# Two encoder layers on one core: the last placements of the recurrence's scores are traced later, and the sums over features are ordered behind the low half of their operand

## The chip, the cores and the metric

One core of a Trainium2 chip runs the whole program in one launch. The time is the device time of one execution in microseconds (us). The kernel before took 1623.28 us (median of 3 runs, 1622.96 to 1624.02).

## The reference

`x` is 512 tokens by 1024 features, and there are two layers. In each, a normed `x` goes through one wide projection (6144 columns) into a differential attention, a bidirectional gated recurrence (HGRN2) and two gates; both branches are projected, gated, summed, projected again and added to `x`; a SwiGLU feed-forward with 2816 hidden units follows. The change touches only the recurrence. For each of its 4 heads (128 features, 512 tokens) and each direction, the reference does this in chunks of 64 tokens:

```python
b = jnp.cumsum(gc, axis=2)
inter = jnp.einsum('bhck,bhkv->bhcv', qc * jnp.exp(b), state)
diff = b[:, :, :, None, :] - b[:, :, None, :, :]
decay = jnp.exp(jnp.where(tril[:, :, None], diff, -jnp.inf))
scores = jnp.einsum('bhtk,bhsk,bhtsk->bhts', qc, kc, decay)
intra = jnp.einsum('bhts,bhsv->bhtv', scores, vc)
```

and sums the outputs of the two directions, norms them over the head's features and multiplies them with a sigmoid gate.

## The kernel before, in words

Everything is feature-major: 128 features on the partitions, 512 tokens along the free axis. The projections split each fp32 operand into a high and a low fp32r half (`hi`, `lo`, or `hh`, `hl`) and run three matmuls per block of 128 features (`mm3`, lines 208 to 210); the high half is made by ScalarE (line 92, a copy), the low half by VectorE (`tt`, line 81, a subtraction). These matmuls are the rows `m<-...`.

`hgrn_head` computes one head. Both directions go through one 128x512 matrix of scores `A` (key tokens by query tokens, in four blocks of 128). As the decay between two tokens cannot be had as a product over a whole chunk, the pairs of tokens are split into levels. Level L (64, 32, 16, 8, 4, 2) covers the pairs that lie in neighbouring blocks of L tokens. `level(L)` makes its two factors in one tile (`fl`): four VectorE subtractions or additions of 128x256 (`subs`), one ScalarE Exp over 128x1024 (`exp`), one VectorE product with `q` of 128x512 (`mult`); at L = 64 the pieces are a little different. `scores` multiplies the factors, four fp32 matmuls of 128x128 into one PSUM bank (`sc`; the trace has two records for each). `place` copies those entries of the bank that belong to the level into `A`: for L of 64, 32 and 16 by ScalarE copies of rectangles (lines 549, 553), and below by one VectorE predicated copy of 128x512 with a mask (line 556). Below level 2 there are two more terms, neighbours (1) and the diagonal (0), which are sums over the features of `kk`: `kk` is split into `kh` (ScalarE, line 574) and `kl` (VectorE, line 575, shown under line 81), each multiplied by a matrix of ones (`nr`, lines 580 and 581: 2 terms x 2 halves, 512 columns each), and placed by two more predicated copies. So a head has five predicated copies: 8, 4, 2, 1, 0. Then `po` (line 593) multiplies `A` and the chunk states with the values.

In this text sc(8), mult(2), place(4) and so on stand for the scores, the product and the placement of a level.

The loop before computes the factors of a level, then the scores of the level before it, and places these at once. After the loop it makes `kh` and `kl`, the scores of level 2, place(2), and the sums.

What sets the order. The instructions are not run in the order in which they are traced. A planner goes through the whole program at compile time, with its own estimates of durations, and for each engine picks among the instructions whose inputs are ready the one traced first; what stands in an `urgent()` block (loads, weight splits and evacuations of the projections) goes ahead. The result is a fixed queue per engine, which the engine works off in order, waiting on semaphores. So the heads, whose instructions depend on each other, are interleaved with projection matmuls that are independent of them. `behind(a, b)` tells the planner to order `a` after `b` although `a` does not use its result; it adds no semaphore. In `scores`, `mark` is the instruction after which the matmuls are ordered: the Exp of the next level, or for level 2 the copy to `kh`.

Two pools matter. The factor tiles (`tag="fac"`) have `FAC` = 4 slots. Two of them hold the factors of the chunk states (`ff`, `fb`) until `po`; the levels, `kh` and `kl` take turns in the other two, so `kl` takes the slot of level 2 and `kh` that of level 4, and the next head's `ff` and `fb` (the rows `fs`) take those of `kh` and `kl`. The PSUM banks of the heads come from a pool of 4 (`pside`). Heads run in two pairs per layer, and the eight heads are counted 0 to 7 here; even heads are first of a pair.

Of the kernel before, what the change touches and what calls it, by code (L numbers as in the profile page):

```python
# [9 lines left out]
F32 = mybir.dt.float32  # L10
# [4 lines left out]
ALU = mybir.AluOpType  # L15
# [32 lines left out]
def kernel(  # L48
# [17 lines left out]
    PE, DVE, ACT, POOL = nc.tensor, nc.vector, nc.scalar, nc.gpsimd  # L66
# [3 lines left out]
    def act(o, i, func, bias=None, scale=None, accum=None):  # L70
        kw = {}
        if bias is not None:
            kw["bias"] = bias
        if scale is not None:
            kw["scale"] = scale
        if accum is not None:
            kw["accum_out"] = accum
        return ACT.activation(o, i, func, **kw)  # L78

    def tt(o, a, b, op):  # L80
        return DVE.tensor_tensor(o, a, b, op)  # L81

    def stt(o, a, s, b, op0, op1):
        return DVE.scalar_tensor_tensor(o, a, s, b, op0, op1)  # L84
# [9 lines left out]
    def behind(ins, other):  # L94

        tc.add_manual_dep(ins.ins, other.ins.name,
                          mybir.DependencyInfo(mybir.DependencyClass.NoSync, mybir.DependencyReason.DATA),
                          reason="keep the tensor engine from waiting")
# [8 lines left out]
    def bank(name="s"):  # L107
        return pside.tile([P, T], F32, tag="s", name=name)

    def mbank(name="m"):  # L110
        return pm.tile([P, T], F32, tag="m", name=name)
# [6 lines left out]
    ones_r = cp.tile([P, P], F32R, name="ones_r")  # L118
# [261 lines left out]
    def sigmoid(v):  # L380

        act(v, v, AF.Exp, scale=-1.0)
        act(v, v, AF.Ln, bias=one)
        return act(v, v, AF.Exp, scale=-1.0)
# [21 lines left out]
    def hgrn_head(l, h, q, z, sg, vB, oh, ol, hgp):  # L406
# [28 lines left out]
        kk = z  # L435
# [47 lines left out]
        def turned(f, kc):  # L483

            pt = bank("kt")
            for i in range(3):
                c = (kc + i) * P
                PE.transpose(pt[:, i * P:(i + 1) * P], f[:, 1, c:c + P], ident)
            kt = hgp.tile([P, 3, P], F32, tag="kt", name="kt")
            return kt, ACT.copy(kt.rearrange("p i c -> p (i c)"), pt[:, :3 * P])  # L490

        def states(d, kt, kc, *marks):
            ps = bank("st")
            for i in range(3):
                mm = PE.matmul(ps[:, i * P:(i + 1) * P], kt[:, i, :], vB[:, kc + i, h * P:(h + 1) * P],
                               start=True, stop=True)
                for mark in marks:
                    behind(mm, mark)
            S = hgp.tile([P, 3, P], F32, tag=f"S{d}", name="S")
            order = (0, 1, 2) if d == 0 else (2, 1, 0)  # L500
            for n, i in enumerate(order):
                if n == 0:
                    DVE.tensor_copy(S[:, i, :], ps[:, i * P:(i + 1) * P])
                else:
                    stt(S[:, i, :], S[:, order[n - 1], :], dec[:, d, kc + i:kc + i + 1],
                        ps[:, i * P:(i + 1) * P], ALU.mult, ALU.add)
            return S

        def level(L):

            f = hgp.tile([P, 2, T], F32, tag="fac", name="fl", bufs=FAC)
            Q, K = blocks(f[:, 0, :]), blocks(f[:, 1, :])
            if L == 64:
                side = lambda v, i: v.rearrange("p (b two) c -> p b two c", two=2)[:, :, i]
                of, ob = [tot[:, d].rearrange("p (b two) -> p b two", two=2)[:, :, 0:1].to_broadcast([P, 4, 64])
                          for d in range(2)]
                act(side(Q, 1), side(cf, 1), AF.Exp)
                act(side(K, 1), side(ab, 1), AF.Exp)
                tt(side(Q, 0), ob, side(xb, 0), ALU.subtract)
                tt(side(K, 0), side(af, 0), of, ALU.add)  # L520
                act(side(Q, 0), side(Q, 0), AF.Exp)
                mark = act(side(K, 0), side(K, 0), AF.Exp)
            else:
                side = lambda v, i: v.rearrange("p b (n two c) -> p b n two c", two=2, c=L)[:, :, :, i]
                mid = lambda v: side(v, 0)[:, :, :, L - 1:L].to_broadcast([P, 8, 32 // L, L])
                of, ob = mid(cf), mid(cb)
                tt(side(Q, 1), side(cf, 1), of, ALU.subtract)
                tt(side(K, 1), side(ab, 1), ob, ALU.subtract)
                tt(side(Q, 0), ob, side(xb, 0), ALU.subtract)
                tt(side(K, 0), side(af, 0), of, ALU.add)  # L530
                mark = act(f, f, AF.Exp)
            tt(f[:, 0, :], f[:, 0, :], q, ALU.mult)
            return f[:, 1, :], f[:, 0, :], mark
# [4 lines left out]
        def scores(K, Q, mark):  # L538
            ps = bank("sc")
            for s in range(TC):  # L540
                c = slice(s * P, (s + 1) * P)
                mm = PE.matmul(ps[:, c], K[:, c], Q[:, c], start=True, stop=True)  # L542
                behind(mm, mark)
            return ps.rearrange("p (i c) -> p i c", c=P), mm

        def place(L, pv):

            if L == 64:
                ACT.copy(A, pv)
            elif L >= 16:  # L550
                for i in range(64 // L):
                    c = slice(i * 2 * L, (i + 1) * 2 * L)
                    ACT.copy(A[c, :, c], pv[c, :, c])
            else:
                j = (2 * L).bit_length() - 1 if L else 0
                DVE.copy_predicated(A, masks[:, j, :].unsqueeze(1).to_broadcast([P, TC, P]), pv)
# [3 lines left out]
        kf, _ = turned(ff, fk)  # L560
        kb, turn = turned(fb, bk)

        done = None
        for L in (64, 32, 16, 8, 4, 2):
            *kq, mark = level(L)
            if L == 32:
                behind(act(dec, suf[:, :, :, 0], AF.Exp), turn)
                S = [states(0, kf, fk, turn, mark), states(1, kb, bk, turn, mark)]
            if done is not None:
                place(done[0], scores(*done[1], mark)[0])  # L570
            done = (L, kq)
        kh = hgp.tile([P, 2, T], F32R, tag="fac", name="kh", bufs=FAC)
        kl = hgp.tile([P, 2, T], F32R, tag="fac", name="kl", bufs=FAC)
        mark = ACT.copy(kh, kk)
        tt(kl, kk, kh.bitcast(F32), ALU.subtract)
        pv, mark = scores(*done[1], mark)
        place(2, pv)
        for i in (1, 0):
            ps = bank("nr")
            behind(PE.matmul(ps, ones_r, kh[:, i, :], start=True, stop=False), mark)  # L580
            PE.matmul(ps, ones_r, kl[:, i, :], start=False, stop=True)
            place(i, ps.rearrange("p (i c) -> p i c", c=P))
        po = bank("po")
        last = None
        for c in range(TC):
            tok = slice(c * P, (c + 1) * P)
            terms = [(vB[:, c, h * P:(h + 1) * P], A[:, c, :])]
            if c < TC - 1:
                terms.insert(0, (S[1][:, c, :], fb[:, 0, tok]))
            if c > 0:  # L590
                terms.insert(0, (S[0][:, c - 1, :], ff[:, 0, tok]))
            for i, (a, b) in enumerate(terms):
# [6 lines left out]
        with tc.issue_after(first.ins):  # L599
            mark = sigmoid(sg)  # L600
# [114 lines left out]
    for l in range(LAYERS):  # L715
        win = w_in[l]
        an = [vecs[:, V_FFN + 8 * l + c:V_FFN + 8 * l + c + 1] for c in range(DC)]
        with ExitStack() as mix:
# [19 lines left out]
            with tc.tile_pool(name=f"hgrn{l}", bufs=2, reuse_waits="tile") as hgp:  # L738
# [22 lines left out]
                def run(h):  # L761
                    hgrn_head(l, h, *heads[h], vB, obh[:, h, :], obl[:, h, :], hgp)
# [59 lines left out]
        with tc.tile_pool(name=f"ffn{l}", bufs=2, reuse_waits="tile") as fp:  # L822
            gh = fp.tile([P, FC, T], F32R, name="gh", bufs=1)
            gl = fp.tile([P, FC, T], F32R, name="gl", bufs=1)
            for f0 in range(0, FC, 2):
# [3 lines left out]
                for f in (f0, f0 + 1):  # L829
                    c0 = slice((f - f0) * P, (f - f0 + 1) * P)  # L830
                    tmp = []
                    for raw in (rg, ru):
                        with urgent():
                            wh, wl = wsplit(raw[:, :, c0])
                        ps = mbank()
# [14 lines left out]
            if l < LAYERS - 1:  # L850
                nn = [vecs[:, V_ATT + 8 * (l + 1) + c:V_ATT + 8 * (l + 1) + c + 1] for c in range(DC)]
                for c0 in range(0, DC, 2):
                    ps = [mbank(), mbank()]
# [16 lines left out]
            else:  # L870
# [10 lines left out]
                ps = [[mbank(), mbank()] if t < 2 else [bank(), bank()] for t in range(TC)]  # L881
# [66 lines left out]
```

## Time and profile before

| | |
|---|---|
| median of 3 runs | 1623.28 us |
| the profiled execution | 1623.66 us, its span 1621.9 us |
| ACT busy, share of the span | 771.6 us, 48% |
| POOL busy | 8.1 us, 1% |
| DMA | 142.53 MB, mean 88 GB/s |
| granted TensorE clock, mean | 0.999 |

The profile shows one execution. PE is the matmul unit, PEld its weight loads, DVE VectorE, ACT ScalarE. PE's busy time counts overlapping matmuls, so a busy PE can still be late; how late is read from the distance between the starts of successive matmuls. A row of the timeline has start, duration, engine, line, operation, and in brackets how long the engine was idle ahead of it and for whom.

### The profile page before, as it was taken

To read this page: it belongs to the slowest core of one execution; us is meant where nothing else is said; L and a number is where in the kernel's file an instruction comes from. 1 tells how busy PE (TensorE), PEld (TensorE's weight loads), DVE (VectorE), ACT (ScalarE), POOL (GpSimd) and SP (SyncE) were. 2 spreads that over 40 slices of the span, in tenths; PEclk is the share of its full clock that TensorE was granted. 3 is DMA by queue.
4 is the path that set the end of the run, shared out by engine and by line. 5 is a ranking of instruction groups with operands and counts; after the bars stand their busy time and mean duration, and the time that the engine had idled before them with its cause. 6 is when DMAs were issued, how large, how long until landed. Compare 5 with 4: busy or idle time off the path is not lost.

```text
span 1621.9 us, 18719 instructions
## 1 busy us (share of the span) xinstructions
PE 1602.1 (99%) x7456; PEld 1323.5 (82%) x7456; DVE 1013.1 (62%) x1636; ACT 771.6 (48%) x1186; POOL 8.1 (1%) x21
## 2 busy tenths in 40 slices
PE   8999999999999999999999999999999999999998
PEld 6888888887888888888888888888878888888886
DVE  8878977877654444433368789788875444444224
ACT  4666666676432323322355667676754323233213
POOL 2000000000000000000000000000000000000000
PEclk9999999999999999999999999999999999999999
DMA  5312212221333223323322222122123233332221
GB/s 189 105 52 79 79 61 70 78 79 52 104 104 92 90 83 99 111 89 100 103 92 83 73 78 79 54 77 79 52 79 97 84 104 104 104 103 92 104 85 72
DMA packets 117927, 142.53 MB, mean 88 GB/s; under 512 B 3152, under 2 KB 100432, under 8 KB 117840
## 3 DMA queue, kind: packets, MB, share of 16 engines
q1 hardware_dynamic: 117152, 140.78, 26.8%
q8 instruction: 58, 0.95, 0.2%
q10 hardware_dynamic: 688, 0.56, 0.1%
q14 instruction: 29, 0.24, 0.0%
HBM read 139.23 MB, written 2.10 MB: 87 GB/s over the span
## 4 chain that ended last, share of the span: by engine, by line
PE 83%; DVE 11%; ACT 4%; issue 1%; DMA 0%; ACTq 0%; DVEq 0%
PE m L210 24%; PE m L208 24%; PE m L209 24%; DVE lo L81 2%; DVE fl L81 2%; PE sc L542 2%; PE s L208 1%; PE s L209 1%; PE s L210 1%; DVE z L81 1%; PE qk L659 1%; PE wt L706 1%; PE po L593 1%; PE qk L656 1%; DVE cum L447 1%
## 5 line engine op out<-in xcount | busy, mean ns | idle before, releaser
L92 ACT CAST hi<-raw 128x1024 fp32r<-128x1024 f32 (+2 forms) x274 | 272.2, 995 | 616.4 <-PE m L209 477.2
L208 PE MATMUL m<-hh,hi 128*128 128x512 f32 x1216 | 476.5, 392 | 5.7 <-DVE hi L289 5.7
L210 PE MATMUL m<-hh,lo 128*128 128x512 f32 x1216 | 476.2, 392 | 0.0
L209 PE MATMUL m<-hl,hi 128*128 128x512 f32 x1216 | 476.1, 392 | 0.0
L81 DVE TENSOR_TENSOR lo<-raw,hi 128x1024 fp32r<-128x1024 f32 (+2 forms) x282 | 320.9, 1139 | 177.5 <-ACT hi L92 176.1
L208 PEld LDWEIGHTS m<-hh,hi 128*128 128x128 f32 x1216 | 228.9, 188 | 52.2 <-ACT sacc L78 5.7
L209 PEld LDWEIGHTS m<-hl,hi 128*128 128x128 f32 x1216 | 228.9, 188 | 47.3 <-DVE hl L84 0.4
L210 PEld LDWEIGHTS m<-hh,lo 128*128 128x128 f32 x1216 | 228.9, 188 | 47.1 <-DVE lo L81 0.3
L81 DVE TENSOR_TENSOR gu<-m,rbc 128x512 f32<-128x512 f32 x88 | 60.9, 692 | 241.2 <-PE m L210 237.2
L208 PE MATMUL m<-hi,hh 128*128 128x512 f32 x256 | 101.4, 396 | 0.0
L209 PE MATMUL m<-lo,hh 128*128 128x512 f32 x256 | 100.9, 394 | 0.0
L210 PE MATMUL m<-hi,hl 128*128 128x512 f32 x256 | 100.9, 394 | 0.0
L78 ACT ACTIVATE fl<-fl 128x1024 f32<-128x1024 f32 (+1 forms) x56 | 48.5, 872 | 43.8 <-DVE fl L81 43.8
L210 PE MATMUL m<-gh,lo 128*128 128x512 f32 x176 | 68.5, 389 | 0.0
L209 PE MATMUL m<-gl,hi 128*128 128x512 f32 x176 | 68.5, 389 | 0.0
L208 PE MATMUL m<-gh,hi 128*128 128x512 f32 x176 | 68.5, 389 | 0.0
L210 PEld LDWEIGHTS m<-hi,hl 128*128 128x128 f32 x256 | 48.2, 188 | 9.6
L542 PEld LDWEIGHTS sc<-fl 128*128 128x128 f32 x384 | 49.0, 191 | 8.5 <-DVE fl L81 4.3
L209 PEld LDWEIGHTS m<-lo,hh 128*128 128x128 f32 x256 | 48.2, 188 | 9.3
L208 PEld LDWEIGHTS m<-hi,hh 128*128 128x128 f32 x256 | 48.2, 188 | 9.3
L542 PE MATMUL sc<-fl 128*128 128x128 f32 x384 | 51.5, 277 | 2.8 <-DVE fl L81 2.6
L209 PE MATMUL m<-ml,hi 128*128 128x512 f32 x128 | 49.8, 392 | 0.0
(255 smaller groups left out, 2340.4 us busy)
## 6 DMA issues: line engine op xcount, KB each, us to landing
raw<-in_w_in_dram SPq DMA_DIRECT2D x46, 1024.0 KB, 5.0
raw<-in_w_gate_dram SPq DMA_DIRECT2D x22, 1024.0 KB, 5.1
raw<-in_w_up_dram SPq DMA_DIRECT2D x22, 1024.0 KB, 5.1
raw<-in_w_down_dram SPq DMA_DIRECT2D x19, 1024.0 KB, 4.9
raw<-in_w_o_dram SPq DMA_DIRECT2D x8, 1024.0 KB, 4.9
raw<-in_w_b_dram SPq DMA_DIRECT2D x4, 1024.0 KB, 5.0
raw<-in_w_a_dram SPq DMA_DIRECT2D x4, 1024.0 KB, 5.0
raw<-in_w_down_dram SPq DMA_DIRECT2D x4, 768.0 KB, 4.2
```

The costliest lines, as they stand in the source:

```text
L78: return ACT.activation(o, i, func, **kw)
L81: return DVE.tensor_tensor(o, a, b, op)
L92: return ACT.copy(hi, src), tt(lo, src, hi.bitcast(F32), ALU.subtract)
L208: PE.matmul(ps, lh, rh, start=start, stop=False)
L209: PE.matmul(ps, lh, rl, start=False, stop=False)
L210: PE.matmul(ps, ll, rh, start=False, stop=stop)
L447: DVE.tensor_tensor_scan(row, seg, row, 0.0, ALU.mult, ALU.add)
L542: mm = PE.matmul(ps[:, c], K[:, c], Q[:, c], start=True, stop=True)
L593: mm = PE.matmul(po[:, tok], a, b, start=i == 0, stop=i == len(terms) - 1)
L656: mm = PE.matmul(ps[c], q2[:, c, tok], ka[:, c, :], start=True, stop=False)
L659: PE.matmul(ps[c], q2[:, c, tok], kb[:, c, :], start=False, stop=True)
L706: tr = PE.transpose(pt[:, s * P:(s + 1) * P], w[:, 0, s * P:(s + 1) * P], ident)
```

## The change

In the loop, a level whose scores are placed by a predicated copy (8 and 4) is no longer placed at once. Its scores are still traced where they were; the placement is kept in `late` and traced in the next round, after the factors of the next level: place(8) after the factors of level 2 in place of after those of level 4, and place(4) after the loop, ahead of `kh`. Levels 64, 32 and 16 are placed as before. The sums over the features are ordered behind the VectorE subtraction that makes `kl`, where they were ordered behind the scores of level 2. No instruction is added or removed.

```diff
-        done = None
+        done = late = None
         for L in (64, 32, 16, 8, 4, 2):
             *kq, mark = level(L)
             if L == 32:
                 behind(act(dec, suf[:, :, :, 0], AF.Exp), turn)
                 S = [states(0, kf, fk, turn, mark), states(1, kb, bk, turn, mark)]
+
+            if late is not None:
+                late = place(*late)
             if done is not None:
-                place(done[0], scores(*done[1], mark)[0])
+                late = (done[0], scores(*done[1], mark)[0])
+                if done[0] >= 16:
+                    late = place(*late)
             done = (L, kq)
         kh = hgp.tile([P, 2, T], F32R, tag="fac", name="kh", bufs=FAC)
         kl = hgp.tile([P, 2, T], F32R, tag="fac", name="kl", bufs=FAC)
+        place(*late)
         mark = ACT.copy(kh, kk)
-        tt(kl, kk, kh.bitcast(F32), ALU.subtract)
-        pv, mark = scores(*done[1], mark)
-        place(2, pv)
+        turn = tt(kl, kk, kh.bitcast(F32), ALU.subtract)
+        place(2, scores(*done[1], mark)[0])
         for i in (1, 0):
             ps = bank("nr")
-            behind(PE.matmul(ps, ones_r, kh[:, i, :], start=True, stop=False), mark)
+            behind(PE.matmul(ps, ones_r, kh[:, i, :], start=True, stop=False), turn)
             PE.matmul(ps, ones_r, kl[:, i, :], start=False, stop=True)
             place(i, ps.rearrange("p (i c) -> p i c", c=P))
```

## Rows read from the trace of the kernel before

**Rows 1.** The page's busy times: busy us, share of the span, instructions.

```profile
PE 1602.1 (99%) x7456; PEld 1323.5 (82%) x7456; DVE 1013.1 (62%) x1636; ACT 771.6 (48%) x1186; POOL 8.1 (1%) x21
```

**Rows 2.** Windows view, heads with attention, then none: us, PE, PEld, DVE, ACT, POOL.

```profile
200.00:400.00 200.00, 198.22 (x949) 162.32 (x948) 155.58 (x273) 134.70 (x242) 0.00 (x0) 1.00 0.20 64
400.00:600.00 200.00, 199.99 (x882) 164.89 (x881) 104.95 (x130) 70.30 (x89) 0.00 (x0) 1.00 0.32 100
```

**Rows 3.** Waits of PE, whole span: us in total, times, longest.

```profile
PE m L208 <- DVE hi L289: 5.7, 1, 5.7
PE sc L542 <- DVE fl L81: 2.6, 3, 1.3
...
PE nr L581 <- DVE kl L81: 0.3, 1, 0.3
```

**Rows 4.** Timeline of PE, end of head 0's levels.

```profile
91.84 0.40 PE L209 MATMUL m<-lo,hh 128*128 128x512 f32 x1
93.56 1.16 PE L542 MATMUL sc<-fl 128*128 128x128 f32 x8 [1.33 <-DVE fl L81]
94.48 0.70 PE L580 MATMUL nr<-kh,ones_r 128*128 128x512 f32 x2
95.02 0.38 PE L593 MATMUL po<-fs,S 128*128 128x128 f32 x2
...
95.47 0.40 PE L208 MATMUL m<-hi,hh 128*128 128x512 f32 x1
95.70 0.40 PE L209 MATMUL m<-lo,hh 128*128 128x512 f32 x1
96.10 0.73 PE L581 MATMUL nr<-kl,ones_r 128*128 128x512 f32 x2
```

**Rows 5.** Timeline of PE, the same places of heads 2, 4 and 6.

```profile
184.75 0.39 PE L209 MATMUL m<-lo,hh 128*128 128x512 f32 x1
186.22 1.13 PE L542 MATMUL sc<-fl 128*128 128x128 f32 x8 [1.08 <-DVE fl L81]
...
893.73 0.40 PE L209 MATMUL m<-lo,hh 128*128 128x512 f32 x1
894.36 1.16 PE L542 MATMUL sc<-fl 128*128 128x128 f32 x8 [0.23 <-DVE fl L81]
...
989.10 0.40 PE L209 MATMUL m<-lo,hh 128*128 128x512 f32 x1
989.59 1.16 PE L542 MATMUL sc<-fl 128*128 128x128 f32 x8
...
992.89 0.39 PE L208 MATMUL m<-hi,hh 128*128 128x512 f32 x1
993.60 0.74 PE L581 MATMUL nr<-kl,ones_r 128*128 128x512 f32 x2 [0.32 <-DVE kl L81]
```

**Rows 6.** Timeline of DVE, head 0, from mult(4) to the next head's first factor.

```profile
88.97 0.68 DVE L81 TENSOR_TENSOR fl<-fl,q 128x512 f32<-128x512 f32 x1
89.58 0.73 DVE L556 COPY_PREDICATED A<-masks,sc 128x512 f32<-128x512 int8 x1
90.20 0.41 DVE L81 TENSOR_TENSOR fl<-cum 128x256 f32<-128x256 f32 x1
...
91.19 0.42 DVE L81 TENSOR_TENSOR fl<-lk,cum 128x256 f32<-128x256 f32 x1
...
92.82 0.69 DVE L81 TENSOR_TENSOR fl<-fl,q 128x512 f32<-128x512 f32 x1 [1.05 <-ACT fl L78]
...
94.82 1.23 DVE L81 TENSOR_TENSOR kl<-z,kh 128x1024 fp32r<-128x1024 f32 x1 [0.67 <-PE sc L542]
...
96.58 0.55 DVE L81 TENSOR_TENSOR fs<-cum,pre 128x384 f32<-128x384 f32 x1
```

**Rows 7.** Timeline of ACT, head 0: exp(2).

```profile
91.73 1.06 ACT L78 ACTIVATE fl<-fl 128x1024 f32<-128x1024 f32 x1 [2.92 <-DVE fl L81]
```

**Rows 8.** Timeline of DVE, head 3 (an odd one): place(4).

```profile
221.14 0.76 DVE L556 COPY_PREDICATED A<-masks,sc 128x512 f32<-128x512 int8 x1 [1.03 <-PE sc L542]
```

## The prediction

> **What bounds the kernel now.** I read the busy times first, then the windows, then the waits of PE, and last the timelines around the levels that the change touches. The busy times give PE 99% of the span [rows 1]. That alone proves little, because overlapping matmuls count as busy. The timeline settles it: successive projection matmuls start 0.23 us apart (95.47 to 95.70) [rows 4], and wherever the distance is longer, the excess is a stall. The windows show that a stretch with heads in it is almost as dense as one with none: PE 198.22 of 200 us against 199.99, although DVE has 155.58 us of work there against 104.95 [rows 2]. So PE works off a fixed amount of matmuls, the heads' DVE and ACT work runs beside projection matmuls, and this change, which adds and removes no instruction, can only move PE's stalls.
>
> PE's waits name those that the change can reach [rows 3]. The largest, 5.7 us, is the first weight of the program and stays. At the scores PE waits 2.6 us in 3 waits for the factors, and at the sums 0.3 us for `kl`. The timelines give the true sizes, with the 0.23 us of a matmul taken off the distance to the one before. Ahead of sc(2): head 0 93.56 - 91.84 - 0.23 = 1.49 us [rows 4], head 2 1.47 - 0.23 = 1.24, head 4 0.63 - 0.23 = 0.40, head 6 0.49 - 0.23 = 0.26 [rows 5]; together 3.39 us. Ahead of the sums' second halves, which read `kl`: 96.10 - 95.70 - 0.23 = 0.17 us in head 0 [rows 4] and 0.71 - 0.23 = 0.48 in head 6 [rows 5]; heads 2 and 4 lie at the size of head 0, four such waits, about 1.0 us. The odd heads show no stall of PE at either place. All that the change can remove directly is therefore 3.39 + 1.0 = 4.4 us, 0.27% of the time.
>
> **The change part by part.**
>
> *Place(8) leaves the chain.* In head 0 DVE runs mult(4) at 88.97, place(8) at 89.58, and the first of subs(2) at 90.20: the copy holds up level 2 by 90.20 - 89.58 = 0.62 us [rows 6]. Then come the last of the subs (91.19), exp(2) on ACT at 91.73 [rows 7], and 1.05 us in which DVE is idle for it, until mult(2) at 92.82 [rows 6]. Traced after the factors of level 2, place(8) has a lower priority than the subs, its scores are long done, and 0.62 us fit into 1.05. So subs(2), exp(2), mult(2) all come 0.62 us earlier and the copy is hidden under exp(2). If that cover went (a weight split taking the idle time), the copy would fall after mult(2), where DVE idles another 0.67 us for sc(2) ahead of `kl` [rows 6]; with that gone too, it would delay `kl` by 0.62 us.
>
> What that is worth on PE is the uncertain step. If PE's queue stayed as it is, each even head's wait would shrink by 0.62 us, or by all of it: 0.62 + 0.62 + 0.40 + 0.26 = 1.90 us. But the queue is planned: the wait exists because the planner thinks that mult(2) is done sooner than it is, and a planner that sees the level end 0.62 us earlier puts sc(2) ahead by as much, with two or three projection matmuls of 0.23 us fewer in front. Then the wait stays at its size and the gain is 0. If the planner counts the copy for more than it takes, sc(2) moves ahead by more than the factors do, and the wait grows; I bound that at one copy per even head, +2.5 us. Between -1.9 and +2.5 I take half of the gain, -0.95 us: the planner's order follows the factors, but the copy is one of the DVE operations on the chain on which it was too optimistic.
>
> *Place(4).* It runs in the idle time ahead of `kl` in even heads and keeps that place. In head 3 it waits 1.03 us for its scores with DVE idle, ahead of mult(2) [rows 8]; there place(8) now fits in. PE has no stall in these heads, so this is worth 0, with DVE's idle time as the only thing that changes.
>
> *The sums behind `kl`.* Before, the two sums over `kh` start as soon as sc(2) is through (94.48), and the two over `kl` at 96.10 [rows 4]. `kl` takes the slot of level 2 and so waits for sc(2): it starts at 94.82 and takes 1.23 us [rows 6]. Afterwards all four sums stand behind `kl`, and PE needs 2 x 0.23 = 0.46 us of other matmuls in their old place. In this stretch projection matmuls are at hand (they stand between `po` and the sums already) [rows 4]. What waits is the same instruction as before, a sum for `kl`, with the same end of `kl`; so I take 0. Bounds: -1.0 us if the planner now places it late enough, and +0.46 us in each of 8 heads, +3.7, if nothing is put in the gap. Queued behind a waiting sum on PE are all projection matmuls that follow; nothing overtakes it.
>
> *What comes free later.* `kh` was read until 94.48 + 0.46 = 94.94; now until about 96.10 + 4 x 0.23 = 97.0. The next head's first factor takes that slot and starts at 96.58 [rows 6], so it starts 0.4 us later, or a DVE operation later. A bank of scores is also held for a level longer. Both delay DVE work of a head whose PE work is interleaved with projections, 0 on PE as long as these last; 0.4 us for each of the four heads that follow in a pair, 1.6 us, if they do not.
>
> The sum: -0.95 + 0 + 0 + 0, about -1.0 us. The profiled execution took 1623.66 us (span 1621.9 and 1.8 outside it), so it would become 1622.7; it lies 0.4 us above the median of the runs, 1623.28, which would become **1622.3 us**. The forecast's own range is 1620.4 (both gains, -1.9 and -1.0) to 1624.9 (no gain, and the late slots, +1.6).
>
> **The rivals.**
>
> *All waits go* (1618.9). The shorter chain and the sums' later place line up so that PE meets its inputs at all eight places: -4.4 us. For it: DVE has the idle time to hide the copy, and 0.40 and 0.26 us are less than one copy. Against it: the waits of heads 0 and 2 are more than twice the 0.62 us that the chain gets shorter.
>
> *The heads' DVE chain sets the pace* (1618.3). If PE's density were an appearance and DVE the real limit, every head would become one copy shorter: 8 x 0.62 = 5.0 us. For it: weight loads fill 162.32 of 200 us with heads and 164.89 without [rows 2], 82% over the span [rows 1], so PE looks far from full. Against it: the 0.23 us between matmuls are the same in the middle of a head. The Trainium skill (Trainium Kernel Development and Optimization, Performance Expectations) says that matmul busy time is a bad measure of how near a kernel is to its limit and that the share of weight loads should be read; by that rule this rival would hold, and the spacing in this trace speaks against it, since the loads show the same share where no head runs.
>
> *The sums' wait takes the place of the one removed* (1626.9, the other side). The planner puts nothing into the old place of the two sums over `kh`, so that PE stands 0.45 us longer for `kl` in each of the 8 heads, +3.6 us, with the gain of place(8) lost to the planner moving sc(2). It decides from about 0.4 us per head, 3.2 us in all. For it: the planner is already too early for `kl` in all four even heads. Against it: projection matmuls are ready there.
>
> *The change does little of what it says* (1623.3). The subtraction to `kl` waits for sc(2) anyway, place(4) has its gap already, and sc(2) is planned ahead with the factors; the queues shift by a few places and the stalls keep their sizes.
>
> **How the numbers follow.** The forecast 0.46, all waits go 0.14, DVE's chain 0.06, the sums' wait 0.16, little done 0.18. About 0.2%, 3.2 us, is what a measurement of this kernel can tell from no change: faster means under 1620.0, slower over 1626.5. Faster is then 0.14 + 0.06 = 0.20, slower 0.16, within 0.46 + 0.18 = 0.64. The range runs from the end of the second rival, 1618.3, to just above the third, 1627.0; outside remain about half of the sums' rival and half of the DVE rival and a little of the first, 0.13 in all.
>
> **What the new profile would show.** Right: on DVE no predicated copy between mult(4) and subs(2) in the even heads, and one in the idle time under exp(2); on PE the waits ahead of sc(2) at or under their old sizes, and projection matmuls between sc(2) and the first sum over `kh`, which starts after `kl`. Wrong: place(8) after mult(2); a wait over 0.4 us ahead of the sums in odd heads too; or new waits of PE at weights (`lo`) or at the chunk states, which no step here has.

## The result and the profile after

The changed kernel takes 1625.86 us (median of 22 runs, 1625.16 to 1627.05) against 1623.49 us of the kernel before (22 runs, 1622.96 to 1624.82): ratio 1.0015, 95% interval 1.0009 to 1.0021. It is slower by 2.4 us, where 1.0 us less was forecast; the time lies inside the range that was given, on the other side of the kernel before. The profiled execution took 1626.06 us, its span 1624.3 us.

The busy times of the changed kernel stand where those of before stood [rows 1]; no engine has more work:

```profile
PE 1603.7 (99%) x7456; PEld 1324.1 (82%) x7456; DVE 1013.8 (62%) x1636; ACT 773.2 (48%) x1186; POOL 8.4 (1%) x21
```

PE's waits of the changed kernel (us in total, times, longest) show where the time went: four waits at the scores in place of three [rows 3], and the transposes of the chunk states, which had 0.2 us before.

```profile
PE sc L542 <- DVE fl L81: 3.0, 4, 1.1
...
PE kt L488 <- ACT fs L78: 1.1, 2, 0.9
```

DVE of head 0 in the changed kernel, to be laid beside [rows 6]. The move is done as predicted: mult(4) at 89.21, the subs directly behind it, place(8) at 91.15 in the idle time under exp(2), mult(2), place(4), `kl`.

```profile
89.21 0.69 DVE L81 TENSOR_TENSOR fl<-fl,q 128x512 f32<-128x512 f32 x1
89.81 0.42 DVE L81 TENSOR_TENSOR fl<-cum 128x256 f32<-128x256 f32 x1
...
91.15 0.74 DVE L556 COPY_PREDICATED A<-masks,sc 128x512 f32<-128x512 int8 x1
...
92.44 0.69 DVE L81 TENSOR_TENSOR fl<-fl,q 128x512 f32<-128x512 f32 x1 [0.53 <-ACT fl L78]
93.05 0.73 DVE L556 COPY_PREDICATED A<-masks,sc 128x512 f32<-128x512 int8 x1
94.44 1.23 DVE L81 TENSOR_TENSOR kl<-z,kh 128x1024 fp32r<-128x1024 f32 x1 [0.66 <-PE sc L542]
```

From mult(4) to mult(2) DVE took 92.82 - 88.97 = 3.85 us before [rows 6] and takes 92.44 - 89.21 = 3.23 now: the 0.62 us came, in full. But PE's queue moved with it. Here are sc(8) and sc(4) of head 0 on PE, first of the kernel before, then of the changed one:

```profile
86.56 1.09 PE L542 MATMUL sc<-fl 128*128 128x128 f32 x8
...
90.25 1.05 PE L542 MATMUL sc<-fl 128*128 128x128 f32 x8
```

```profile
87.53 1.06 PE L542 MATMUL sc<-fl 128*128 128x128 f32 x8
...
90.50 1.05 PE L542 MATMUL sc<-fl 128*128 128x128 f32 x8
...
92.09 0.40 PE L209 MATMUL m<-lo,hh 128*128 128x512 f32 x1
93.19 1.16 PE L542 MATMUL sc<-fl 128*128 128x128 f32 x8 [0.70 <-DVE fl L81]
94.10 0.48 PE L210 MATMUL m<-hi,hl 128*128 128x512 f32 x1
94.42 0.62 PE L585 MATMUL nr<-kh,ones_r 128*128 128x512 f32 x2
...
95.34 0.40 PE L209 MATMUL m<-lo,hh 128*128 128x512 f32 x1
95.72 0.73 PE L586 MATMUL nr<-kl,ones_r 128*128 128x512 f32 x2
```

Between them stand 12 projection matmuls before (3.69 us) and 9 now (2.97 us); sc(2) follows 4 matmuls after sc(4) in both. So the planner counted the copy at three matmuls, 0.7 us, and drew the scores ahead by that. The sums over `kh` begin at 94.42, one matmul behind sc(2) and as early as `kl` itself (94.44), and so in all heads but head 6. To the planner, "behind" is behind the start of the other instruction, and the prediction had read it as behind its end.

The other heads at sc(2), PE of the changed kernel, in the order of heads 2, 4, 6 and 7 [rows 5 for the first three]:

```profile
187.46 0.39 PE L209 MATMUL m<-lo,hh 128*128 128x512 f32 x1
188.95 1.16 PE L542 MATMUL sc<-fl 128*128 128x128 f32 x8 [1.09 <-DVE fl L81]
...
894.03 0.40 PE L209 MATMUL m<-lo,hh 128*128 128x512 f32 x1
894.73 1.16 PE L542 MATMUL sc<-fl 128*128 128x128 f32 x8 [0.31 <-DVE fl L81]
...
992.89 0.40 PE L208 MATMUL m<-hi,hh 128*128 128x512 f32 x1
994.14 1.13 PE L542 MATMUL sc<-fl 128*128 128x128 f32 x8 [0.85 <-DVE fl L81]
...
1028.90 0.39 PE L210 MATMUL m<-hh,lo 128*128 128x512 f32 x1
1029.37 1.16 PE L542 MATMUL sc<-fl 128*128 128x128 f32 x8
```

With 0.23 us taken off each distance, the waits went in head 2 from 1.24 to 1.26 us, in head 4 from 0.40 to 0.47, in head 6 from 0.26 to 1.02; head 7 has 0.24 where it had none.

### The profile page after: what moved, and what is told of

Its sections match the earlier page's. It is cut to its first block, busy times and chain, and to the rows that moved or that the text cites. A ratio compares the mean times of both kernels' runs of the same rounds, so it can differ in the third digit from the quotient of the medians.

```text
span 1624.3 us, 18713 instructions
## 1 busy us (share of the span) xinstructions
PE 1603.7 (99%) x7456; PEld 1324.1 (82%) x7456; DVE 1013.8 (62%) x1636; ACT 773.2 (48%) x1186; POOL 8.4 (1%) x21
## 4 chain that ended last, share of the span: by engine, by line
PE 85%; DVE 9%; ACT 5%; issue 1%; DMA 0%; ACTq 0%; DVEq 0%
PE m L210 24%; PE m L208 24%; PE m L209 24%; DVE fl L81 2%; DVE lo L81 2%; PE sc L542 2%; PE po L598 1%; ACT hi L92 1%; PE s L208 1%; PE s L209 1%; PE s L210 1%; PE qk L664 1%; PE wt L711 1%; ACT lk L78 1%; PE qk L661 1%
```

## The experiments

All were timed in five rounds, with the kernel before on the same chip (1623.59 us for the changed kernel once more, each half alone and sc(2) held back, 1623.63 for the others). This table holds the medians and, from each profile, PE's waits in us, worked out as above: ahead of sc(2), ahead of the sums over `kl`, and, where they are 0.09 us or more, at the transposes and state products of the chunk states. Head 0's part of the column sc(2) depends on the start of the execution as well: it is 0.87 and 1.31 us in two profiles of the changed kernel.

| kernel | median | ratio to before, 95% | sc(2) | sums | chunk states |
|---|---|---|---|---|---|
| before | 1623.5 | | 3.4 | 1.0 | 0.9 |
| changed | 1625.86 | 1.0009 to 1.0021 | 4.1 | 1.1 | 1.7 |
| the changed once more | 1625.67 | 1.0005 to 1.0022 | 4.5 | 1.1 | 1.7 |
| place(8) later alone | 1625.78 | 1.0005 to 1.0022 | 4.1 | 1.1 | 1.7 |
| sums behind `kl` alone | 1623.65 | 0.9992 to 1.0010 | 3.3 | 1.0 | 0.9 |
| changed, sc(2) held back | 1623.01 | 0.9987 to 1.0005 | 0.4 | 2.2 | 2.0 |
| before, place(4) behind mult(2) | 1626.37 | 1.0008 to 1.0025 | 3.5 | 1.2 | 1.9 |
| before, sums behind place(2) | 1622.99 | 0.9988 to 1.0006 | 2.8 | 0.3 | 0.9 |
| changed, sums behind place(2) | 1625.14 | 1.0003 to 1.0021 | 5.1 | 0 | 1.3 |
| changed, both held back | 1621.43 | 0.9979 to 0.9997 | 1.0 | 0.6 | 0.8 |

**The changed kernel once more.** No edit.

> The changed kernel once more, for a second profile of it. In its first profile TensorE's clock rose at 12.2 us, in that of the kernel before at 9.6 us, which cost PE 1.24 us at the very start. My theory: that moment moves from execution to execution and is not the change's, and where it falls late, head 0's wait ahead of sc(2) is shorter by what PE came late; with an early rise the wait of 0.87 us should be near 1.9 us, with a late one near 0.9, and all other waits of the heads should repeat within 0.1 us: sc(2) 1.26 (head 2), 0.48 (head 4), 1.02 (head 6), 0.24 (head 7). Time 1625.9. Rival: the late rise is part of the change (another order of the first instructions); then the rise is at 12.2 us again.

The step came early: matmuls start 0.43 us apart up to 9.13 in the second profile, and up to 12.18 in the first, with no change in the program. What the rows show is a step in the spacing; a rise of the granted clock they do not show (last section). The second profile first, then the first:

```profile
8.70 0.63 PE L208 MATMUL m<-hh,hi 128*128 128x512 f32 x1
9.13 0.46 PE L209 MATMUL m<-hl,hi 128*128 128x512 f32 x1
9.43 0.39 PE L210 MATMUL m<-hh,lo 128*128 128x512 f32 x1
...
91.25 0.40 PE L209 MATMUL m<-lo,hh 128*128 128x512 f32 x1
92.79 1.16 PE L542 MATMUL sc<-fl 128*128 128x128 f32 x8 [1.15 <-DVE fl L81]
```

```profile
11.75 0.60 PE L209 MATMUL m<-hl,hi 128*128 128x512 f32 x1
12.18 0.40 PE L210 MATMUL m<-hh,lo 128*128 128x512 f32 x1
12.42 0.40 PE L208 MATMUL m<-hh,hi 128*128 128x512 f32 x1
```

Head 0 then waits 92.79 - 91.25 - 0.23 = 1.31 us where it waited 0.87; of the rest of the 1.9 that was expected, 0.16 us stands ahead of its sc(4) and 0.10 ahead of its sc(16), and the remainder is not there. The other waits repeat to 0.01 us. This profile, which starts like that of before, can be laid beside it: sc(2) 4.54 - 3.39 = 1.15, sums 0.11, transposes of head 6 1.04 - 0.38 = 0.66, together 1.92 us, and the two profiled times differ by 1625.59 - 1623.66 = 1.93 us. That the two agree so closely is luck in part: smaller terms are left out and cancel, among them head 2's transposes, which wait 0.40 us more, and its state products and head 6's output products, which wait 0.2 us less each.

**Each half alone.** Place(8) later, with the sums as before:

```diff
-        turn = tt(kl, kk, kh.bitcast(F32), ALU.subtract)
-        place(2, scores(*done[1], mark)[0])
+        tt(kl, kk, kh.bitcast(F32), ALU.subtract)
+        pv, turn = scores(*done[1], mark)
+        place(2, pv)
```

> One half of the change alone: place(8) is traced after the factors of level 2, the sums over the features stay ordered behind the scores of level 2. My theory: the planner counts a predicated copy at about what it takes and moves sc(4) and sc(2) ahead with the shorter chain, by three projection matmuls in head 0 (12 to 9 between sc(8) and sc(4)) and by two to four ahead of sc(2) in the odd heads; so the waits ahead of sc(2) stay in the even heads, new ones come in the odd heads, and this half carries the whole loss: 1625.9, within 0.4. Rival one, the sums carry it: then this half is at or below the kernel before, 1622.5 to 1623.5. Rival two, both halves carry it: 1624.7.

And the sums behind `kl`, with the placements as before:

```diff
-        tt(kl, kk, kh.bitcast(F32), ALU.subtract)
-        pv, mark = scores(*done[1], mark)
-        place(2, pv)
+        turn = tt(kl, kk, kh.bitcast(F32), ALU.subtract)
+        place(2, scores(*done[1], mark)[0])
...
-            behind(PE.matmul(ps, ones_r, kh[:, i, :], start=True, stop=False), mark)
+            behind(PE.matmul(ps, ones_r, kh[:, i, :], start=True, stop=False), turn)
```

> The other half alone: the sums are ordered behind the start of the subtraction that makes kl, the placements stay where they were before. My theory: in the even heads this moves the two sums over kh by one projection matmul, in the odd heads by six where PE has no wait; the wait of the sums over kl stays at 0.17 us in the even heads. 1623.5, within 0.4 of the kernel before. Rival one, the sums carry the loss (PE stands for kl in all eight heads, 0.3 us each): 1625.9. Rival two, both halves carry it: 1624.7.

1625.78 and 1623.65: the later placement carries the whole loss, and the order of the sums is worth nothing that can be measured. The rivals in which the sums carry it, alone or in part, fall.

**Sc(2) held back in the changed kernel.**

```diff
-                late = place(*late)
+                behind(place(*late), level.product)
...
-        place(*late)
-        mark = ACT.copy(kh, kk)
+        mark = place(*late)
+        ACT.copy(kh, kk)
```

(`level.product` is mult of the level just made, and `place` now returns its copy.)

> The changed kernel with one more delay that my theory needs: place(8) is ordered behind mult(2), place(4) follows it, and sc(2) is ordered behind place(4), so that the planner puts sc(2) one predicated copy (about 0.6 us, three projection matmuls) later on PE while its factors are ready as early as in the changed kernel. My theory (PE waits because the planner puts sc(2) earlier than its factors are there): the waits ahead of sc(2) fall by 0.6 to 0.7 us or to nothing, from about 1.9, 1.26, 0.48 and 1.02 us in the even heads and 0.07 to 0.24 in the odd ones; 2.5 to 3 us less than the changed kernel, 1623.1. Rival, the recurrence's own chain sets the pace of PE: sc(2) later by 0.6 us in eight heads makes it slower, up to 1630.7, and never faster than 1625.9.

1623.01, 2.7 us below the changed kernel in the same rounds (1625.24 to 1626.36 there, 1622.18 to 1623.87 here). In head 0, PE and DVE of this kernel:

```profile
92.67 0.39 PE L209 MATMUL m<-lo,hh 128*128 128x512 f32 x1
93.09 1.16 PE L542 MATMUL sc<-fl 128*128 128x128 f32 x8
```

```profile
92.34 0.69 DVE L81 TENSOR_TENSOR fl<-fl,q 128x512 f32<-128x512 f32 x1 [1.06 <-ACT fl L78]
92.95 1.56 DVE L556 COPY_PREDICATED A<-masks,sc 128x512 f32<-128x512 int8 x2
```

Mult(2) starts about when it did in the changed kernel (92.34 and 92.44), but 7 matmuls stand between sc(4) and sc(2) in place of 4, and the wait is 93.09 - 92.67 - 0.23 = 0.19 us. All sc(2) waits together fall to 0.4 us. Delaying an instruction on PE made the program faster, which no pace set by the recurrence's chain would allow; PE waits because its queue reaches sc(2) too early. Some of it comes back as waits for `kl`, 2.2 us in place of 1.1, and at the chunk states, 2.0 in place of 1.7.

**The odd heads' gap, in the kernel before.**

```diff
-                place(done[0], scores(*done[1], mark)[0])
+                put = place(done[0], scores(*done[1], mark)[0])
+                if L == 2:
+                    behind(put, level.product)
```

> The kernel before with one order more: place(4) is ordered behind mult(2). Nothing moves in the even heads, where it is there already; in the odd heads place(4) no longer stands in DVE's queue ahead of mult(2), as in the changed kernel. My theory: place(4) in that gap made the planner put sc(2) and the sums of the odd heads late enough; without it the number of projection matmuls ahead of sc(2) falls from 7 to 4 in heads 1, 3, 5 and 7, and PE gets waits of 0.1 to 0.25 us ahead of sc(2) and of 0.15 us ahead of the sums over kl there: 0.25 to 0.4 us in each of four heads, 1624.5 to 1625.1. Rival: the odd heads have slack and lose nothing, the loss of the change lies in head 6 and in the transposes of the chunk states alone; then 1623.5.

1626.37. With place(4) out of the gap, head 3 of this kernel waits on PE at both places (0.44 - 0.23 = 0.21 us and 0.39 - 0.23 = 0.16 us):

```profile
227.28 0.40 PE L209 MATMUL m<-hl,hi 128*128 128x512 f32 x1
227.72 1.13 PE L542 MATMUL sc<-fl 128*128 128x128 f32 x8
...
229.83 0.40 PE L209 MATMUL m<-hl,hi 128*128 128x512 f32 x1
230.22 0.73 PE L583 MATMUL nr<-kl,ones_r 128*128 128x512 f32 x2
```

In the kernel before the same two places have 0.23 us from start to start, no wait:

```profile
222.33 0.39 PE L210 MATMUL m<-hh,lo 128*128 128x512 f32 x1
222.56 1.12 PE L542 MATMUL sc<-fl 128*128 128x128 f32 x8
...
225.82 0.39 PE L209 MATMUL m<-hl,hi 128*128 128x512 f32 x1
226.04 0.71 PE L581 MATMUL nr<-kl,ones_r 128*128 128x512 f32 x2
```

The direction is the one expected, the size is not: 2.7 us, where 0.9 to 1.5 were. Heads 1, 3 and 5 lie in the expected size or just under it (0.33 to 0.37 us each); head 7 has 0.67 ahead of sc(2), and 1.0 us more than before lies at the chunk states. In heads 0 and 2, where nothing was to move, sc(2) waits 0.7 and 0.4 us less. One order changed in four heads re-planned what came after them. The size of 2.7 us is also not all in these waits: in this profile the first matmul starts at 6.36 us, in the nine others at 5.70 to 5.77, and the spacing steps late, at 12.31. What either is worth in the median is not known. So this run shows the odd heads' waits, and not what they cost in time.

**The sums held back.** The sums are ordered behind place(2), which follows `kl` on DVE; first in the kernel before, then in the changed one, then in the changed one with sc(2) held back. The edit in the changed kernel:

```diff
-        turn = tt(kl, kk, kh.bitcast(F32), ALU.subtract)
-        place(2, scores(*done[1], mark)[0])
+        tt(kl, kk, kh.bitcast(F32), ALU.subtract)
+        turn = place(2, scores(*done[1], mark)[0])
```

> The kernel before with the sums over the features ordered behind place(2), which stands behind the subtraction that makes kl in DVE's queue. My theory: the planner then puts the sums after the end of kl and not only after its start, with the two sums over kh ahead of those over kl as a margin of 0.46 us; the waits ahead of the sums over kl (0.17, 0.17, 0.17 and 0.48 us) go: 1622.6. Rival: place(1), place(0), the end of the head and the slots of kh and kl come later, and PE waits for the next head instead: 1623.5 to 1626.

> The changed kernel with the sums ordered behind place(2) in place of behind the start of the subtraction that makes kl. My theory: only the waits ahead of the sums over kl go, 0.16 us in seven heads; the waits ahead of sc(2) stay: 1625.7 - 1.1 = 1624.6. Rival: the later end of the heads eats it, 1625.7 or more.

> The changed kernel with both margins: sc(2) ordered behind place(4), which follows place(8) behind mult(2), and the sums behind place(2). My theory: with the first margin alone the time was 1623.0, and its profile still has waits ahead of the sums over kl of 0.17 to 0.23 us in seven heads and 0.93 in head 6, 2.2 us together; without them 1620.8, faster than both kernels. Rival: the later end of the heads eats it, 1623.0 or more.

The waits ahead of the sums go in all heads but head 6, and there too in the changed kernel. In the kernel before that is 1622.99, 0.6 us less, within the interval of no change; in the changed one 1625.14, as sc(2) waits 0.3 us longer in head 6 and 0.15 in heads 1 and 5, and sc(4) of head 2 got a wait of 0.34 us. With both orders 1621.43 (0.9979 to 0.9997): faster than both kernels, if by 0.6 us less than expected. Its waits (`po` is the output product of a head):

```profile
PE sc L542 <- DVE fl L81: 0.6, 1, 0.6
PE nr L587 <- DVE kl L81: 0.5, 1, 0.5
...
PE po L599 <- DVE A L556: 0.2, 1, 0.2
```

What is left at the places of the change is one wait at sc(2) in head 2 (0.71 us), one for `kl` in head 6 (0.63 us), and 0.27 us at sc(2) in head 0. New are waits at `po` for the last placements, 0.1 to 0.4 us in five heads, 0.9 us together, where the changed kernel and the one with sc(2) alone held back have none: there the rival, that the later end of the heads eats the gain, is right in part.

## Why the prediction was wrong

**What bounds the kernel: right.** PE's work did not change, and the time followed PE's stalls: three of them come to 1.92 us in the second profile of the changed kernel, which took 1.93 us longer, with smaller ones that cancel. The rival with DVE's chain as the pace is out, as the chain got shorter by 0.62 us and the time longer, and with sc(2) later the time fell.

**Place(8) leaves the chain: the step that failed.** The prediction had the bound right, "a planner that sees the level end 0.62 us earlier puts sc(2) ahead by as much ... and the gain is 0", and then took half of the gain, -0.95 us, on the ground that the copy was one of the operations on which the planner was too optimistic. Nothing had shown that of the copy. The planner counted it at about what it takes (three matmuls of 0.23 us for 0.62), and with starts alike (the second profile) the waits of heads 0, 2 and 4 went by -0.18, +0.02 and +0.07 us: the term was -0.1 there, and with the +0.76 of head 6 it was +0.7 over the four even heads, not -0.95. In head 6 the cover was lost to what had been named, a weight split, which took DVE behind place(8). DVE and then ACT of the changed kernel:

```profile
991.55 0.74 DVE L556 COPY_PREDICATED A<-masks,sc 128x512 f32<-128x512 int8 x1
992.18 1.21 DVE L81 TENSOR_TENSOR lo<-raw,hi 128x1024 fp32r<-128x1024 f32 x1
993.31 0.68 DVE L81 TENSOR_TENSOR fl<-fl,q 128x512 f32<-128x512 f32 x1
```

```profile
991.73 1.06 ACT L78 ACTIVATE fl<-fl 128x1024 f32<-128x1024 f32 x1 [0.55 <-DVE fl L81]
```

Exp(2) ends at 991.73 + 1.06 = 992.79, mult(2) starts at 993.31: half a microsecond of the 0.76 by which head 6's wait grew. In the kernel before, mult(2) of this head started 0.14 us after exp(2). The prediction put the price of a lost cover on `kl`, not on mult(2) in front of it.

**Place(4) in the odd heads: failed too.** "PE has no stall in these heads, so this is worth 0." They had none because place(4) stood ahead of mult(2) [rows 8] and the planner put sc(2) later for it, 7 matmuls behind sc(4). With place(8) in that gap there are 5, 3, 5 and 3, and the heads wait 0.07 to 0.24 us at sc(2) and 0.15 or 0.16 at the sums: +1.1 us over four heads. The run with place(4) alone behind mult(2) shows such waits with place(8) where it was. A place without a wait was read as slack; it was margin, and the change took it away.

**The sums: right in size, wrong in how.** The term was 0, and the run with this half alone took 1623.65 us against 1623.59, with 1.0 us of waits ahead of the sums as before. The bound of 0.46 us per head was not reached: the planner let the sums over `kh` start with `kl` and not after it.

**What comes free later: 0 was taken, on the wrong place.** It looked at slots and banks alone. PE's transposes in head 6 waited 1.04 us (0.38 before) for the first factors' Exp, which stood on ACT behind a weight split. PE, then ACT, of the changed kernel:

```profile
968.33 0.39 PE L209 MATMUL m<-lo,hh 128*128 128x512 f32 x1
969.60 0.55 PE L488 MATMUL kt<-ident,fs 128*128 128x128 f32 x3 [0.89 <-ACT fs L78]
```

```profile
968.10 1.03 ACT L92 CAST hi<-raw 128x1024 fp32r<-128x1024 f32 x1
969.03 0.93 ACT L78 ACTIVATE fs<-fs 128x384 f32<-128x384 f32 x2
```

The kernels with place(8) later have this wait at 0.8 to 1.0 us, but for the last one (0.31), and so has the one with place(4) behind mult(2); the two with only the sums moved keep 0.38. No run moved it alone, so which order makes it stays open. The prediction had named new waits at the chunk states as a sign that it was wrong.

The sum, with starts alike: heads 0, 2 and 4 -0.1, head 6 +0.76 at sc(2) and -0.48 at the sums, odd heads +1.1, transposes +0.66: +1.9 us of the 2.1 to 2.4 measured, with the smaller terms that cancel left out. The forecast missed by 3.3 us; of these the half gain that was taken is 0.85, the odd heads' margin 1.1, and head 6 with its transposes 0.94; the remaining 0.4 us was not traced.

**The other rivals.** The time came out next to the third rival's 1626.9, and not for its reason: it wanted 0.45 us for `kl` in each of the 8 heads, and PE waits 0.15 or 0.16 us in seven, with the sums ordered as before too. What the fourth rival said of the queue, that sc(2) is planned ahead with the factors, is what heads 0, 2 and 4 show; it missed what the odd heads and head 6 lost.

## What to carry to other kernels

Where a planner fixes the queues, a wait on the engine that sets the time is the gap between the planner's estimate and the chip; making the chain ahead of it shorter by an operation that the planner prices rightly moves the waiting instruction ahead as well and gains nothing. Hold the waiting instruction back by an order of its own, and take a spot that has no wait for margin until the row shows by how much its inputs were early. Before any order is changed, ask whether it is on the start or on the end of the other instruction.

## What was not expected of the hardware

The first projection matmuls start 0.43 us apart and later ones 0.23 us; the step came at 9.57 us in the kernel before, and at 12.18 and 9.13 us in two profiles of one and the same changed program, while the windows view gives a granted clock of 1.00, that is 2.4 GHz, on both sides of it in all three. Here are two stretches of the changed kernel's first profile, ahead of the step and past it; the granted clock stands third from the end, in front of the DMA share and GB/s:

```profile
10.50:12.00 1.50, 1.50 (x5) 1.21 (x4) 1.50 (x4) 1.01 (x2) 0.00 (x0) 1.00 1.07 382
12.00:14.00 2.00, 2.00 (x9) 1.60 (x9) 2.00 (x5) 1.25 (x2) 0.00 (x0) 1.00 1.00 324
```

In the ten profiles of this case the step lies between 9.13 and 12.31 us. It moves up to 1.4 us of PE's time from execution to execution (the 61st matmul of the changed program starts at 22.66 us in one profile and at 21.24 in the other), and part of it is taken back at a later wait, head 0's sc(2), which was 0.87 us with the late step and 1.31 us with the early one.
